# Down-projection units issued one pair of hidden tiles later, with two of four weight-block sums made by adding DMAs

## The chip, the cores and the metric

The kernel runs on one core of a Trainium2 chip. The metric is device time in microseconds (us) of one execution of the whole kernel, a decoder layer on 512 tokens of width 1024. Several executions are timed, and the median is given. Beside these there is one profiled execution, from which the trace and its page come.

## What is computed

The layer has two feed-forward blocks, one at its start and one at its end, with a token mixer and a memory attention between them. Only the feed-forward blocks are touched by the change:

```python
def swiglu(x, w1, w3, w2):
    return (jax.nn.silu(x @ w1) * (x @ w3)) @ w2

h = layer_norm(ALPHA * h + 0.5 * swiglu(h, ffn1_w1[l], ffn1_w3[l], ffn1_w2[l]), ln1_g[l], ln1_b[l])
...
h = layer_norm(ALPHA * h + 0.5 * swiglu(h, ffn2_w1[l], ffn2_w3[l], ffn2_w2[l]), ln4_g[l], ln4_b[l])
```

All is float32. `h` is 512 x 1024, `w1` and `w3` are 1024 x 2816, and `w2` is 2816 x 1024. The 2816 hidden columns are 22 tiles of 128, which the kernel takes in 11 pairs.

## The kernel before, in words

**Exact products.** A float32 operand is split into a high part and a low part in `float32r` (`split`: the copy that rounds, then a subtraction for the rest), and each product is three matmuls (`mm3`). The copy may go to ACT or to DVE (`scaled`), the subtraction is always on DVE. So every weight tile passes through DVE before TensorE can use it.

**Seven products in place of eight.** In the feed-forward blocks a 2 x 2 block product is done in Winograd's form with seven block products and sums of blocks. `Unit` (line 485) makes the seven weight forms of one unit, numbered 1 to 7, out of four loaded blocks of 128 x 1024: block 0 alone is form 1, block 2 form 2, block 3 form 3, and forms 5, 6, 7 and 4 are sums, made on DVE in place (block 0 takes in 1, then 3, then 2, and block 1 takes in 3). `Weights` keeps at most five such split tiles (`hl`) ahead of the product that TensorE is at, and `Unit.make` starts the loads of the unit after it at its fourth and its sixth form.

**Two kinds of units.** An up unit (`seven`, `products`) makes one pair of hidden tiles, with 7 products of 24 matmuls of 256 columns. Its outputs pass through ACT (silu) and DVE into a tile `G`. A down unit (`Forms`, `down7`) takes two pairs `G`, forms seven operands `A1` to `A7` out of their blocks (four of them sums on DVE, all split like weights), and makes 7 products of 12 matmuls of 512 columns, in banks dx, dy and dz. There are five down units, g = 0 to 4, over pairs 0 to 9; pair 10 goes through a plain product with `w2` (`res.add`), which ends the block and starts its layer norm.

**Order.** Pair 0 is made in another way at the block's start. Then the program issues, for g = 0 to 4, the up units of pairs 2g and 2g + 1, then down unit g, then the up unit of pair 10:

```python
        for g in range(5):
            if g:
                yield from seven(2 * g)
            forms = Forms(g)
            yield from seven(2 * g + 1, {4: lambda: forms.make(1, 2)})
            yield from down7(g, forms)
```

So down unit g follows at once on the up unit whose `G` it reads. The operands A1 and A2 are asked for ahead of the last product of that up unit, and the others inside the down unit.

**Sums over the down units.** `add` (line 716) takes each product out of its banks. For g = 0 it goes, added to the old residual, into four tiles `acc` in DRAM. For g = 1 to 4 ACT copies it to a staging tile `st` and POOL issues a DMA that adds it to `acc`; adds to the same `acc` wait for one another. `load_acc` reads `acc` back ahead of the fifth product of the up unit of pair 10, for the last sums.

**What sets the order on the engines.** A planner in the program (`Issue`) decides in which order DVE, ACT, POOL and SP (which issues the loads) get their instructions, by its own costs; each engine then works strictly in that order. All loads into SBUF go through SP's one queue. The blocks, `G`, `A`, `st` and `acc` share 20 slots of 4 KB per partition (`arena`), so a load waits where its slot is still in use. Small tables for the mixer (`tables`, line 1390) are made in the middle of the first block.

Of the kernel before, what the change touches and what calls it, by code (L numbers as in the profile page):

```python
# [13 lines left out]
ALU = mybir.AluOpType  # L14
# [4 lines left out]
P = 128  # L19
# [175 lines left out]
def layer(ctx: ExitStack, tc: tile.TileContext, a: dict, out: bass.AP):  # L195
# [247 lines left out]
    class Residual:  # L443
# [5 lines left out]
        def load(self):  # L449
            self.acc = [slot(f"acc{self.n}_{t}", F32, [P, D]) for t in range(NT)]  # L450
            for t in range(NT):
                sp.dma_start(self.acc[t], self.src[t * P:(t + 1) * P])
# [32 lines left out]
    class Unit:  # L485
# [2 lines left out]

        def __init__(self, name, src, order):
            self.name, self.src, self.order, self.after, self.b = name, src, order, None, {}  # L490

        def load(self, *blocks):
            for i in blocks:
                if i not in self.b:
                    self.b[i] = slot(f"{self.name}_b{i}", F32, [P, 1024])
                    for w in range(2):
                        sp.dma_start(self.b[i][:, w * 512:w * 512 + 512], self.src[i][w])

        def plan(self):
            for i in self.order:  # L500
# [2 lines left out]
        def make(self, i, hl):  # L503
            b, at = self.b, self.order.index(i)
            if at == 0:
                self.load(0, 1, 3, 2)
            if self.after and at in (3, 5):
                self.after.load(*((0, 1) if at == 3 else (3, 2)))
            for at, other in {5: ((0, 1),), 6: ((0, 3),), 7: ((1, 3),), 4: ((0, 2),)}.get(i, ()):
                dve.tensor_tensor(b[at], b[at], b[other], op=ALU.add)  # L510
            src = b[{1: 0, 5: 0, 6: 0, 4: 0, 3: 3, 7: 1, 2: 2}[i]]
            split(hl[:, 0], hl[:, 1], src)
            if i == 4:
                b.clear()

# [84 lines left out]
    def plan_ffn(n, w1, w3, w2):  # L600
        for f in range(2):
            W.plan(f"w1_{n}_{f}", w1[f])
            W.plan(f"w3_{n}_{f}", w3[f])

        def up(p):
            return Unit(f"wp{n}_{p}", [[w[2 * p + i % 2][:, i // 2 * 512:i // 2 * 512 + 512] for w in (w1, w3)] for i in range(4)], ORDER)

        def down(g):
            return Unit(f"wd{n}_{g}", [[w2[f * P:(f + 1) * P, i % 2 * 512:i % 2 * 512 + 512] for f in (4 * g + i // 2 * 2, 4 * g + i // 2 * 2 + 1)]
                                       for i in range(4)], DOWN)  # L610

        units = [up(1), down(0)]
        for g in range(1, 5):
            units += [up(2 * g), up(2 * g + 1), down(g)]
        units.append(up(10))
        for u, v in zip(units, units[1:]):
            u.after = v
        for u in units:
            u.plan()
        for f in (20, 21):  # L620
            W.plan(f"w2_{n}_{f}", w2[f * P:(f + 1) * P])

    def ffn(n, src, ready=None):
# [82 lines left out]
        def down7(g, forms):  # L706
# [7 lines left out]
                W.done(f"wd{n}_{g}_{i}")  # L714

            def add(pss, h, c, sign, new=False):
                if g == 0 and new:
                    st = old.pop((h, c))
                    for t in range(2):
                        dve.scalar_tensor_tensor(st[:, t], st[:, t], ALPHA, pss[t], op0=ALU.mult, op1=ALU.add if sign > 0 else ALU.subtract)  # L720
# [7 lines left out]
            x = [bank(f"dx{n}_{g}_{t}") for t in range(2)]  # L728
            product(x, 1, True)
            add(x, 0, 0, 1.0, True)  # L730
            forms.make(5, 6)
            yield
            y = [bank(f"dy{n}_{g}_{t}") for t in range(2)]
            product(y, 2, True)
# [32 lines left out]
            mark = sums_of_h(n, sums)  # L767
            yield from up(range(2))
        yield mark
        load_old()  # L770
        for g in range(5):
            if g:
                yield from seven(2 * g)
            forms = Forms(g)
            yield from seven(2 * g + 1, {4: lambda: forms.make(1, 2)})
            yield from down7(g, forms)

        def load_acc():
            res.acc = [slot(f"acc{n}_{t}", F32, [P, D]) for t in range(NT)]
# [1 line left out]
                for c in range(2):  # L781
                    sp.dma_start(res.acc[t][:, c * 512:c * 512 + 512], acc[t // 2, c][t % 2 * P:t % 2 * P + P])

        yield from seven(10, {7: load_acc})
        yield from res.add(lambda i, t: hl_of(gT[20 + i], slice(t * P, (t + 1) * P)), [f"w2_{n}_{f}" for f in (20, 21)], False, True)


# [707 lines left out]
```

## Time and profile before

| | us |
|---|---|
| median of 3 runs (1308.3 to 1309.8) | 1308.88 |
| profiled execution, its time | 1306.86 |
| profiled execution, its span | 1305.0 |
| first feed-forward block, first up unit to the first product of the mixer | 33.5 to 389.3 |
| mixer and memory attention | 389.3 to 954.7 |
| second block, first up unit to the end | 954.7 to 1305.0 |

Shares of the span in which an engine is busy: TensorE (PE) 94%, VectorE (DVE) 80%, ScalarE (ACT) 42%, GpSimd (POOL) 8%. These are averages over stages that differ; in both feed-forward blocks DVE is near its limit while TensorE has short pauses. Times in the trace are from the span's start. The page leaves out buffer numbers, so `wp_b` are the blocks of all up units and `wd_b` those of all down units. Almost all work has the line of a helper (L178 records it, L260 is the matmul), so it is told apart by its tiles.

### The profile page before, as it was taken

The page shows a single profiled execution, that of the slowest core. Times are in us where ns is not written, and L with a number is a line of the kernel's source. Part 1 is how long each engine was busy: PE and PEld are TensorE (multiplying, and loading weights), DVE is VectorE, ACT ScalarE, POOL GpSimd, SP SyncE. Part 2 cuts the span into 40 slices and gives each one's busy share as a digit, 9 for nine tenths or more (in the row PEclk, how much of TensorE's full clock was granted, in tenths as well). Part 3 has the DMA queues.
Part 4 walks back from the last instruction along what each step waited for, and adds up shares of the span by engine and source line. Part 5 has one row for each costly group of instructions (what it writes and reads, how often), then busy time and mean ns, then how long its engine had stood idle before and what let it go on. Part 6 is the DMA issues. An engine that isn't in the chain of part 4 may idle for free.

```text
span 1305.0 us, 19366 instructions
## 1 busy us (share of the span) xinstructions
PE 1229.0 (94%) x7530; PEld 1079.6 (83%) x7530; DVE 1038.6 (80%) x1603; ACT 551.3 (42%) x977; POOL 99.4 (8%) x95
## 2 busy tenths in 40 slices
PE   7898989899969999999999999999998989899995
PEld 6898988788859987877778898888996979797975
DVE  8999898789873699666666684574999898998987
ACT  5253434353532377433441243451544353535352
POOL 0010202020201100000000000000001020202020
PEclk9999999899989999999999999999999999999998
DMA  9381929484853321242333445234735474748374
GB/s 335 124 261 39 256 61 216 101 198 110 154 177 94 110 72 33 62 133 85 94 98 97 178 162 161 67 128 161 253 118 152 156 182 126 194 114 203 104 127 147
DMA packets 82879, 184.14 MB, mean 141 GB/s; under 512 B 8259, under 2 KB 10051, under 8 KB 82788
## 3 DMA queue, kind: packets, MB, share of 16 engines
q1 hardware_dynamic: 65924, 150.40, 34.3%
q0 software_dynamic: 16864, 32.51, 14.9%
q8 instruction: 59, 0.97, 0.3%
q14 instruction: 32, 0.26, 0.1%
HBM read 137.13 MB, written 45.74 MB: 140 GB/s over the span
## 4 chain that ended last, share of the span: by engine, by line
PE 70%; DVE 19%; DMA 4%; ACT 3%; issue 3%; SPq 0%; POOL 0%; DVEq 0%; POOLq 0%; ACTq 0%
PE pxwp L260 13%; PE pzwp L260 7%; DVE wd_hl L178 6%; PE dx L260 6%; PE dz L260 4%; PE mq L260 3%; PE res_w_o L260 3%; PE pgd L260 3%; PE res_mem_w_o L260 3%; DVE wd_b L178 2%; PE pywp L260 2%; PE pw L260 2%; PE mk L260 2%; PE vd L260 2%; PE pw_gm L260 2%
## 5 line engine op out<-in xcount | busy, mean ns | idle before, releaser
L178 DVE TENSOR_TENSOR wp_hl<-wp_b,wp_hl 128x1024 fp32r<-128x1024 f32 x140 | 168.9, 1222 | 15.6 <-ACT wp_hl L178 14.7
L178 ACT CAST wp_hl<-wp_b 128x1024 fp32r<-128x1024 f32 x88 | 92.1, 1052 | 82.1 <-PE pxwp L260 34.9
L260 PE MATMUL dx<-wd_hl,A 128*128 128x512 f32 x480 | 121.7, 399 | 2.4 <-DVE A L178 1.1
L170 POOL DMA_DIRECT2D acc<-st x62 | 77.6, 1478 | 600.5 <-ACT st L178 435.1
L260 PE MATMUL pxwp<-hT,wp_hl 128*128 128x256 f32 x960 | 121.1, 282 | 1.1 <-ACT wp_hl L178 0.4
L260 PE MATMUL pzwp<-S,wp_hl 128*128 128x256 f32 x960 | 121.8, 283 | 0.3 <-DVE S L178 0.3
L260 PE MATMUL pxwp<-S,wp_hl 128*128 128x256 f32 x960 | 122.0, 283 | 0.0
L260 PEld LDWEIGHTS pxwp<-hT,wp_hl 128*128 128x128 f32 x960 | 117.1, 188 | 5.5 <-DVE p_wp L178 2.1
L260 PEld LDWEIGHTS pzwp<-S,wp_hl 128*128 128x128 f32 x960 | 117.9, 191 | 0.5 <-DVE S L178 0.5
L260 PEld LDWEIGHTS pxwp<-S,wp_hl 128*128 128x128 f32 x960 | 118.1, 191 | 0.2 <-ACT p_wp L178 0.2
L260 PEld LDWEIGHTS dx<-wd_hl,A 128*128 128x128 f32 x480 | 88.9, 190 | 26.6 <-DVE A L178 7.6
L178 DVE TENSOR_TENSOR wd_hl<-wd_b,wd_hl 128x1024 fp32r<-128x1024 f32 x70 | 85.0, 1223 | 16.5 <-ACT wd_hl L178 16.3
L178 DVE TENSOR_TENSOR wp_b<-wp_b,wp_b 128x1024 f32<-128x1024 f32 x80 | 97.5, 1221 | 0.3
L260 PE MATMUL dz<-wd_hl,A 128*128 128x512 f32 x240 | 62.6, 400 | 12.2 <-ACT A L178 12.2
L260 PEld LDWEIGHTS dz<-wd_hl,A 128*128 128x128 f32 x240 | 43.7, 189 | 27.4 <-ACT A L178 15.9
L260 PE MATMUL pywp<-hT,wp_hl 128*128 128x256 f32 x480 | 60.0, 280 | 0.3 <-ACT wp_hl L178 0.3
L260 PE MATMUL dy<-wd_hl,A 128*128 128x512 f32 x120 | 37.1, 460 | 22.7 <-ACT A L178 17.7
L260 PEld LDWEIGHTS pywp<-hT,wp_hl 128*128 128x128 f32 x480 | 58.0, 188 | 0.5 <-ACT wp_hl L178 0.5
L260 PE MATMUL pw<-hT,w_hl 128*128 128x256 f32 (+1 forms) x288 | 50.2, 335 | 6.6 <-ACT hT L178 6.4
L260 PEld LDWEIGHTS pw<-hT,w_hl 128*128 128x128 f32 x288 | 43.0, 197 | 13.1 <-ACT hT L178 7.1
L260 PEld LDWEIGHTS dy<-wd_hl,A 128*128 128x128 f32 x120 | 24.9, 219 | 34.2 <-ACT A L178 21.5
L178 ACT ACTIVATE st<-dx 128x512 f32<-128x512 f32 x68 | 39.8, 598 | 22.9 <-PE dx L260 22.7
(329 smaller groups left out, 2332.0 us busy)
## 6 DMA issues: line engine op xcount, KB each, us to landing
wp_b<-in_ffn_w SPq DMA_DIRECT2D x160, 256.0 KB, 5.6
acc<-st POOLq DMA_DIRECT2D x62, 512.0 KB, 9.5
wd_b<-in_ffn_w SPq DMA_DIRECT2D x80, 256.0 KB, 6.8
h_dram<-acc SPq DMA_DIRECT2D x12, 512.0 KB, 3.0
w_raw<-in_ffn_w SPq DMA_DIRECT2D x11, 512.0 KB, 5.0
w_gm_raw<-in_w_gate SPq DMA_DIRECT2D x8, 512.0 KB, 5.8
acc<-old SPq DMA_DIRECT2D x8, 512.0 KB, 4.2
acc<-acc SPq DMA_DIRECT2D x16, 256.0 KB, 5.6
```

The costliest lines, as they stand in the source:

```text
L170: return (name, 1000.0, 4000.0, lambda: getattr(engine, op)(*args, **kw)), args[:1], list(args)
L178: return (name, ns, 1500.0 if name == "sync" else 0.0, lambda: getattr(engine, op)(*args, **kw)), outs, ins
L260: issue.pe(lambda: nc.tensor.matmul(ps, w, x, start=start, stop=stop, skip_group_check=again), ps, w, x)
```

## The change

- The order becomes: for g = 0 to 4 the up units of pairs 2g + 1 and 2g + 2, then down unit g. A down unit now reads two pairs of which the later was finished one up unit before. `res.add` for pair 10 follows on down unit 4, and no up unit stands between them.
- The operands A1, A2 and A5 are asked for inside the second up unit, ahead of its products 3, 2 and 4.
- Down unit 4 adds its products straight into the `acc` tiles in SBUF on DVE. Its 7 adding DMAs and 14 ACT copies per block are gone, and 14 additions of 128 x 512 on DVE are there. `load_acc` moves to the head of the up unit of pair 10.
- A down unit loads five blocks where it loaded four: block 4 is a second copy of block 0. POOL issues two DMAs that add in SBUF: block 1 from DRAM onto block 4 (form 5) and block 3 onto block 1 (form 7). Of the four sums on DVE two are left (forms 6 and 4). Each block is one DMA of 512 KB in place of two of 256 KB.
- In up units the blocks are loaded in the order 1, 0, 3, 2, where it was 0, 1, 3, 2.

```diff
@@ Unit @@
+            self.adds = not isinstance(src[0], list)
+
+        def move(self, i, block, add=False):
+            src = self.src[i]
+            if add:
+                pool.dma_start(block.rearrange("p (w c) -> p w c", w=2), src, accum_op=ALU.add)
+            elif isinstance(src, list):
+                for w in range(2):
+                    sp.dma_start(block[:, w * 512:w * 512 + 512], src[w])
+            else:
+                sp.dma_start(block.rearrange("p (w c) -> p w c", w=2), src)
 
         def load(self, *blocks):
+
             for i in blocks:
-                if i not in self.b:
+                if i not in self.b and (i < 4 or self.adds):
                     self.b[i] = slot(f"{self.name}_b{i}", F32, [P, 1024])
-                    for w in range(2):
-                        sp.dma_start(self.b[i][:, w * 512:w * 512 + 512], self.src[i][w])
+                    self.move(i % 4, self.b[i])
+                    if self.adds and i in (1, 4):
+                        self.move(3 if i == 1 else 1, self.b[i], True)
...
             if at == 0:
-                self.load(0, 1, 3, 2)
+                self.load(4, 1, 0, 3, 2)
             if self.after and at in (3, 5):
-                self.after.load(*((0, 1) if at == 3 else (3, 2)))
-            for at, other in {5: ((0, 1),), 6: ((0, 3),), 7: ((1, 3),), 4: ((0, 2),)}.get(i, ()):
-                dve.tensor_tensor(b[at], b[at], b[other], op=ALU.add)
-            src = b[{1: 0, 5: 0, 6: 0, 4: 0, 3: 3, 7: 1, 2: 2}[i]]
+                self.after.load(*((4, 1, 0) if at == 3 else (3, 2)))
+            t = 4 if self.adds else 0
+            src = b[{1: 0, 5: t, 6: t, 4: t, 3: 3, 7: 1, 2: 2}[i]]
+            other = {5: 1, 6: 3, 7: 3, 4: 2}.get(i)
+            if other is not None and not (self.adds and i in (5, 7)):
+                dve.tensor_tensor(src, src, b[other], op=ALU.add)
             split(hl[:, 0], hl[:, 1], src)
+            if i == 1 and self.adds:
+                del b[0]
@@ plan_ffn @@
-        units = [up(1), down(0)]
-        for g in range(1, 5):
-            units += [up(2 * g), up(2 * g + 1), down(g)]
-        units.append(up(10))
+        units = []
+        for g in range(5):
+            units += [up(2 * g + 1), up(2 * g + 2), down(g)]
@@ ffn: down7 @@
             def add(pss, h, c, sign, new=False):
-                if g == 0 and new:
+                if g == 4:
+                    for t in range(2):
+                        dst = res.acc[2 * h + t][:, c * 512:c * 512 + 512]
+                        dve.tensor_tensor(dst, dst, pss[t], op=ALU.add if sign > 0 else ALU.subtract)
+                elif g == 0 and new:
...
-            forms.make(5, 6)
+            forms.make(6)
@@ ffn: the order @@
         for g in range(5):
-            if g:
-                yield from seven(2 * g)
+            yield from seven(2 * g + 1)
             forms = Forms(g)
-            yield from seven(2 * g + 1, {4: lambda: forms.make(1, 2)})
+            late = {3: lambda: forms.make(1), 2: lambda: forms.make(2), 4: lambda: forms.make(5)}
+            if g == 4:
+                late[1] = load_acc
+            yield from seven(2 * g + 2, late)
             yield from down7(g, forms)
...
-        yield from seven(10, {7: load_acc})
```

Three places show how the instructions move.

**VectorE, first block, around the start of down unit 2.** The names are tile, block, unit: `wd1_2_b1` is block 1 of down unit 2, `wd1_2_7_hl` its split form 7, `G1_5` the output of the up unit of pair 5, `A2_1_2` the operand A2, `Sa` to `Sd` the sums for the operands. Before:

```order
L178 TENSOR_TENSOR wd1_2_3_hl_1822<-wd1_2_b3_1627,wd1_2_3_hl_1822 128x1024
L178 TENSOR_TENSOR wd1_2_b1_1560<-wd1_2_b1_1560,wd1_2_b3_1627 128x1024
L178 SCALAR_TENSOR_TENSOR G1_5_1600<-p1_wp1_5_1629,G1_5_1600 128x256
L178 CAST wd1_2_7_hl_1843<-wd1_2_b1_1560 128x1024
L178 SCALAR_TENSOR_TENSOR G1_5_1600<-pxwp1_5_1601,G1_5_1600 128x256
L178 TENSOR_TENSOR A2_1_2_1797<-G1_5_1600,A2_1_2_1797 128x2x256
L178 TENSOR_TENSOR wd1_2_7_hl_1843<-wd1_2_b1_1560,wd1_2_7_hl_1843 128x1024
L178 TENSOR_TENSOR wd1_2_b0_1559<-wd1_2_b0_1559,wd1_2_b2_1628 128x1024
L178 TENSOR_TENSOR Sa_1_2_1847<-G1_5_1600,G1_4_1375 128x512
L178 CAST wd1_2_4_hl_1878<-wd1_2_b0_1559 128x1024
L178 TENSOR_TENSOR Sd_1_2_1906<-G1_4_1375 128x512
L178 TENSOR_TENSOR A5_1_2_1848<-Sa_1_2_1847,A5_1_2_1848 128x2x256
```

With the change:

```order
L178 TENSOR_TENSOR Sa_1_2_2023<-G1_5_1597,G1_4_1190 128x512
L178 TENSOR_TENSOR wd1_2_1_hl_1916<-wd1_2_b0_1783,wd1_2_1_hl_1916 128x1024
L178 SCALAR_TENSOR_TENSOR Sb_1_2_2076<-Sa_1_2_2023,G1_4_1190 128x512
L178 CAST wd1_2_2_hl_1946<-wd1_2_b2_1852 128x1024
L178 TENSOR_TENSOR u2_wp1_6_1917<-u2_wp1_6_1917,pzwp1_6_1861 128x512
L178 TENSOR_TENSOR wd1_2_2_hl_1946<-wd1_2_b2_1852,wd1_2_2_hl_1946 128x1024
L178 SCALAR_TENSOR_TENSOR G1_6_1824<-u2_wp1_6_1917,G1_6_1824 128x256
L178 CAST wd1_2_5_hl_1976<-wd1_2_b4_1781 128x1024
L178 TENSOR_TENSOR A2_1_2_1983<-G1_5_1597,A2_1_2_1983 128x2x256
L178 TENSOR_TENSOR wd1_2_5_hl_1976<-wd1_2_b4_1781,wd1_2_5_hl_1976 128x1024
L178 TENSOR_TENSOR p5_wp1_6_1887<-p5_wp1_6_1887,pxwp1_6_1825 128x512
L178 TENSOR_TENSOR wd1_2_b4_1781<-wd1_2_b4_1781,wd1_2_b3_1851 128x1024
```

Before, A2 and the sum Sa stand behind the last write of `G1_5`, and the sums of blocks 1 and 0 between them; now Sa, Sb and A2 stand among the weights of the down unit, `G1_6` is written for a later unit, and form 5 is split out of block 4 with no sum on DVE.

**TensorE, first block, its end.** `res1_w2` are the last products, with the token tile and the half behind them; `trh1` are the transposes of the normed tiles, one token tile each, and `pw_gm` the first products of the mixer, whose first half needs token tiles 0 and 1 only. Before:

```order
L260 MATMUL res1_w2_1_20_3_0_3636<-w2_1_20_hl_3390,g1_20_3531 128x512 x3
L260 MATMUL res1_w2_1_20_3_0_3636<-w2_1_21_hl_3421,g1_21_3456 128x512 x3
L260 MATMUL res1_w2_1_20_3_1_3646<-w2_1_20_hl_3390,g1_20_3531 128x512 x3
L260 MATMUL res1_w2_1_20_3_1_3646<-w2_1_21_hl_3421,g1_21_3456 128x512 x3
L269 MATMUL trh1_1_0_3680<-ident_84,acc1_1_3427 128x128 x4
L269 MATMUL trh1_1_1_3685<-ident_84,acc1_1_3427 128x128 x4
L269 MATMUL trh1_2_0_3697<-ident_84,acc1_2_3428 128x128 x4
L269 MATMUL trh1_2_1_3702<-ident_84,acc1_2_3428 128x128 x4
L260 MATMUL pw_gm0_3671<-hT0_89,w_gm0_hl_3455 128x256
L260 MATMUL pw_gm1_3672<-hT0_89,w_gm1_hl_3497 128x256
```

With the change:

```order
L260 MATMUL res1_w2_1_20_3_1_3604<-w2_1_20_hl_3424,g1_20_3351 128x512 x3
L260 MATMUL res1_w2_1_20_3_1_3604<-w2_1_21_hl_3446,g1_21_3282 128x512 x3
L269 MATMUL trh1_0_0_3637<-ident_84,acc1_0_3119 128x128 x4
L269 MATMUL trh1_0_1_3642<-ident_84,acc1_0_3119 128x128 x4
L269 MATMUL trh1_1_0_3651<-ident_84,acc1_1_3120 128x128 x4
L269 MATMUL trh1_1_1_3657<-ident_84,acc1_1_3120 128x128 x4
L269 MATMUL trh1_2_0_3681<-ident_84,acc1_2_3121 128x128 x4
L269 MATMUL trh1_2_1_3686<-ident_84,acc1_2_3121 128x128 x4
L269 MATMUL trh1_3_0_3695<-ident_84,acc1_3_3122 128x128 x4
L269 MATMUL trh1_3_1_3700<-ident_84,acc1_3_3122 128x128 x4
L260 MATMUL pw_gm0_3625<-hT0_89,w_gm0_hl_3469 128x256 x12
```

Before, the transposes of tiles 0 to 2 are mixed with the last products and the mixer starts ahead of those of tile 3; now all transposes stand in a row behind the last product, and the mixer starts behind the last of them.

**POOL, first block, the adding DMAs between down units 1 and 2** (`acc1_0_1` is the tile in DRAM for token half 0 and column half 1). Before:

```order
L170 DMA acc1_0_1_115<-st1_1_0_1_1296 128x2x512
L170 DMA acc1_0_1_115<-st1_1_0_1_1320 128x2x512
L170 DMA acc1_1_1_117<-st1_1_1_1_1342 128x2x512
L170 DMA acc1_1_0_116<-st1_1_1_0_1368 128x2x512
L170 DMA acc1_0_0_114<-st1_2_0_0_1846 128x2x512
L170 DMA acc1_0_0_114<-st1_2_0_0_1879 128x2x512
```

With the change:

```order
L170 DMA acc1_0_1_115<-st1_1_0_1_1521 128x2x512
L170 DMA acc1_0_1_115<-st1_1_0_1_1544 128x2x512
L170 DMA acc1_1_1_117<-st1_1_1_1_1566 128x2x512
L170 DMA acc1_1_0_116<-st1_1_1_0_1590 128x2x512
L170 DMA wd1_2_b4_1781<-in_ffn1_w2 128x2x512
L170 DMA wd1_2_b1_1782<-in_ffn1_w2 128x2x512
L170 DMA acc1_0_0_114<-st1_2_0_0_2075 128x2x512
```

The two adds for the weights of down unit 2 stand behind all adds of down unit 1 and ahead of those of unit 2.

## Rows read from the trace of the kernel before

**Rows 1.** The page: its head and the busy time of each engine.

```profile
span 1305.0 us, 19366 instructions
...
PE 1229.0 (94%) x7530; PEld 1079.6 (83%) x7530; DVE 1038.6 (80%) x1603; ACT 551.3 (42%) x977; POOL 99.4 (8%) x95
```

**Rows 2.** Stretches: stretch, length, PE, PEld, DVE, ACT, POOL busy (count); PEclk, DMA, GB/s.

```profile
144.00:184.00 40.00, 39.91 (x335) 39.67 (x334) 35.12 (x42) 12.82 (x20) 4.04 (x3) 1.00 0.62 177
184.00:208.00 24.00, 20.70 (x90) 15.58 (x89) 23.31 (x29) 14.75 (x25) 4.81 (x4) 1.00 0.61 123
248.00:279.00 31.00, 26.08 (x103) 20.00 (x102) 27.91 (x34) 15.50 (x26) 5.06 (x4) 0.83 0.57 159
```

**Rows 3.** Timeline of TensorE: first or last products of up units (start, length, what).

```profile
33.52 3.01 PE L260 MATMUL pxwp<-hT,wp_hl 128*128 128x256 f32 x24
...
144.15 3.02 PE L260 MATMUL pxwp<-hT,wp_hl 128*128 128x256 f32 x24
...
208.21 3.02 PE L260 MATMUL pxwp<-hT,wp_hl 128*128 128x256 f32 x24
...
360.00 2.98 PE L260 MATMUL pxwp<-hT,wp_hl 128*128 128x256 f32 x24
...
954.73 3.01 PE L260 MATMUL pxwp<-hT,wp_hl 128*128 128x256 f32 x24
...
1277.49 2.98 PE L260 MATMUL pxwp<-hT,wp_hl 128*128 128x256 f32 x24
```

**Rows 4.** Timeline of TensorE in down unit 2 of the first block [idle before].

```profile
184.46 1.07 PE L260 MATMUL dx<-wd_hl,A 128*128 128x512 f32 x4
...
189.53 3.03 PE L260 MATMUL dy<-wd_hl,A 128*128 128x512 f32 x12 [1.72 <-ACT A L178]
...
194.00 3.21 PE L260 MATMUL dz<-wd_hl,A 128*128 128x512 f32 x12 [1.43 <-ACT A L178]
```

**Rows 5.** Chain of waits, in order of time, in two down units (start, length, what).

```profile
187.36 1.13 DVE wd_b L178
...
264.93 2.73 PE dz L260 x12
```

**Rows 6.** Groups by line and tile: count | busy us, mean ns | idle before.

```profile
L178 DVE TENSOR_TENSOR wd_b<-wd_b,wd_b 128x1024 f32<-128x1024 f32 x40 | 48.8, 1223 | 0.3
...
L178 DVE CAST wd_hl<-wd_b 128x1024 fp32r<-128x1024 f32 x45 | 30.9, 690 | 0.0
...
L178 DVE SCALAR_TENSOR_TENSOR acc<-acc,res_w 128x512 f32<-128x512 f32 x16 | 10.9, 683 | 5.0 <-PE res_w L260 5.0
```

**Rows 7.** Issue to landing: first adds acc<-st (512 KB), then loads wd_b (256 KB).

```profile
DMA to landing us min/median/max: 5.8/9.5/15.7
...
DMA to landing us min/median/max: 3.9/6.8/15.0
```

**Rows 8.** POOL: its adds by group, then its timeline near the end of down unit 2.

```profile
L170 POOL DMA_DIRECT2D acc<-st x62 | 77.6, 1478 | 600.5 <-ACT st L178 435.1 <-DMA acc<-st 67.5 <-ACT A L178 64.1
...
201.09 1.20 POOL L170 DMA_DIRECT2D acc<-st  x1 [0.70 <-ACT st L178]
...
212.50 4.04 POOL L170 DMA_DIRECT2D acc<-st  x3 [10.21 <-ACT wp_hl L178]
```

**Rows 9.** Timelines of SP, PE and DVE at the ends of both blocks.

```profile
337.85 21.25 SPq L178 DMA_DIRECT2D acc<-acc  x8
...
369.78 10.10 PE L260 MATMUL res_w<-w_hl,g 128*128 128x512 f32 x36 [6.80 <-DVE g L178]
...
373.54 0.69 DVE L178 SCALAR_TENSOR_TENSOR acc<-acc,res_w 128x512 f32<-128x512 f32 x1 [3.09 <-PE res_w L260]
...
389.28 7.32 PE L260 MATMUL pw_gm<-hT,w_gm_hl 128*128 128x256 f32 x60
...
396.54 1.09 PE L269 MATMUL trh<-ident,acc 128*128 128x128 f32 x8
...
1284.01 0.69 DVE L178 SCALAR_TENSOR_TENSOR acc<-acc,res_w 128x512 f32<-128x512 f32 x1 [1.48 <-PE res_w L260]
```

More of the change, by code (lines that the diff above doesn't have):

```diff
@@ L608, in down @@
         def down(g):
-            return Unit(f"wd{n}_{g}", [[w2[f * P:(f + 1) * P, i % 2 * 512:i % 2 * 512 + 512] for f in (4 * g + i // 2 * 2, 4 * g + i // 2 * 2 + 1)]
-                                       for i in range(4)], DOWN)
-        units = [up(1), down(0)]
-        for g in range(1, 5):
-            units += [up(2 * g), up(2 * g + 1), down(g)]
-        units.append(up(10))
+            rows = [w2[f * P:(f + 2) * P].rearrange("(f p) c -> p f c", p=P) for f in (4 * g, 4 * g + 2)]
+            return Unit(f"wd{n}_{g}", [rows[i // 2][:, :, i % 2 * 512:i % 2 * 512 + 512] for i in range(4)], DOWN)
+        units = []
+        for g in range(5):
+            units += [up(2 * g + 1), up(2 * g + 2), down(g)]
         for u, v in zip(units, units[1:]):
@@ L769, in ffn @@
         yield mark
-        load_old()
-        for g in range(5):
-            if g:
-                yield from seven(2 * g)
-            forms = Forms(g)
-            yield from seven(2 * g + 1, {4: lambda: forms.make(1, 2)})
-            yield from down7(g, forms)
         def load_acc():
@@ L782, in load_acc @@
                     sp.dma_start(res.acc[t][:, c * 512:c * 512 + 512], acc[t // 2, c][t % 2 * P:t % 2 * P + P])
-        yield from seven(10, {7: load_acc})
+        load_old()
+        for g in range(5):
+            yield from seven(2 * g + 1)
+            forms = Forms(g)
+            late = {3: lambda: forms.make(1), 2: lambda: forms.make(2), 4: lambda: forms.make(5)}
+            if g == 4:
+                late[1] = load_acc
+            yield from seven(2 * g + 2, late)
+            yield from down7(g, forms)
         yield from res.add(lambda i, t: hl_of(gT[20 + i], slice(t * P, (t + 1) * P)), [f"w2_{n}_{f}" for f in (20, 21)], False, True)
```

## The prediction

> **What bounds the kernel now.** I read first the busy time of each engine [rows 1]. TensorE is busy for 1229.0 of 1305.0 us, so at most 76 us of pauses are to be had in the whole kernel. DVE's 80% is an average and hides its stages, so the second view is that of the stretches [rows 2]. While two up units run (144 to 184), TensorE is busy for 39.91 of 40 us and DVE for 35.12: the products are the bound. In the down unit behind them (184 to 208) TensorE is busy for only 20.70 of 24 us, and DVE for 23.31: there DVE is the bound. The third view, TensorE's timeline of that down unit [rows 4], says what the pauses wait for: dy waits 1.72 us and dz 1.43 us for an `A`, together 3.15 of the 3.3 us of pause. The chain of waits [rows 5] runs at that moment through a weight-block sum on DVE (1.13 us at 187.36). So the operands A2 and A5 are late, since `G` of the up unit just before ends with that unit, and their sums then queue on DVE between the splits and sums of the weights. The clock adds to it: in the stretch from 248 to 279, another down unit, the granted clock is 0.83, and it takes 31 us in place of 24 [rows 2].
>
> **How much is lost.** Two up units take 184.46 - 144.15 = 40.31 us [rows 3, 4], 20.16 each. A product of a down unit that waits for nothing takes 2.73 us [rows 5], seven 19.11. A period of two up units and one down unit would be 59.43 us; it is 208.21 - 144.15 = 64.06 us [rows 3]. A block has ten up units and five down units from the first up unit to the last product of pair 10: 10 x 20.16 + 5 x 19.11 = 297.1 us. The first block takes 33.52 to 362.98, 329.5 us, the second 954.73 to 1280.47, 325.7 us [rows 3]. Lost are 32.4 and 28.6 us, 61.0 in all, about 6 per down unit.
>
> **The order: later down units.** The later `G` that a down unit reads is now complete one up unit (20 us) before it begins, and the operands 1, 2 and 5 are made inside that up unit. The waits for `A` should go, and with them the slower clock that followed. The amount of work is the same; it moves out of the stretch in which DVE is full into one where it had 40 - 35.12 = 4.9 us free.
>
> **DVE.** Its load in a period was 35.12 + 23.31 = 58.4 us [rows 2]. Two sums of 1.223 us go, 2.4 us [rows 6]. In the new order of DVE and ACT, 27 copies of down weights move from DVE to ACT and 13 of up weights come back, 14 fewer over ten periods, at 0.690 us [rows 6] 1.0 us each period. Left are 55.0 of 59.4 us, 93%: it fits, with 4.4 us free. ACT takes those copies with some 27 of 59 us in use now (12.82 + 14.75), so I cost them at nothing; if ACT had no room, the price would be the copies' 1.0 us a period again. As DVE works strictly in order and is still at 93%, I do not give the whole loss back: I leave the length of one sum, 1.2 us, in each of the ten down units, 12 us. The bounds are 0 (nothing waits) and 3.0 (half of the loss stays).
>
> **The adding DMAs.** No DMA of the trace before adds onto a weight block; the nearest rows are the adds to `acc`, of the same 512 KB and issued by POOL too. They land after 5.8 to 15.7 us, median 9.5, and loads of blocks after 3.9 to 15.0, median 6.8 [rows 7]. Count from T, the end of a down unit (208.21). Its fourth add is issued at 201.09 [rows 8], lands at T + 2.4 and frees the staging slots; the block loads, issued at about T + 4, land at T + 11. POOL takes its queue in order: the last adds of the down unit end at 212.50 + 4.04, T + 8.3 [rows 8], so the two new ones wait for the loads alone. Issued at T + 12, they land at T + 22. Form 5, the first that needs one, may be split five products ahead of its own, which is when four products of the second up unit are done: T + 20.16 + 4 x 2.88 = T + 31.7. The margin is 9.7 us; I cost the DMAs at nothing, hidden by the up units. With the longest times of the rows for both steps they land at T + 4 + 15.0 + 1.2 + 15.7 = T + 36, 4 us late, still within the 4.4 us that DVE has free. The further bound is the rival below. SP is asked for the same loads plus one block more per unit, 512 KB, while the DMA engines are busy at about 0.6 [rows 2].
>
> **Down unit 4 and the ends of the blocks.** Its 14 additions on DVE (0.683 us, by the nearest row, which also reads a bank [rows 6]) are 9.6 us; the weights of a next up unit, which DVE made there in the other periods, are not there. I take 1 us for them in the second block. In the first, the span from the last product of pair 10 to the mixer's first product was 389.28 - 362.98 = 26.3 us, of which 6.80 was a wait for `g` [rows 9], in a time when SP was held for 21.25 us by the reload of `acc`; that reload is now asked for ahead of down unit 4. What remains counts from the end of down unit 4: first sum of `acc` after 3.76 us (369.78 to 373.54), from there to the transposes of the last token tile 23.0 us (to 396.54), and these 1.09, since the mixer now stands behind them: 27.9 us. That is 1.6 more; 1.1 comes back, as those transposes interrupted the mixer before. For the additions and two splits of mixer weights that stand ahead on DVE (2 x 1.22) I add 2.5. So the first end loses 3.0 us and the second 1.0. The bounds for both are a gain of 2 (the wait of 6.80 was worth more) and a loss of 10 (the 9.6 us of additions all come late once).
>
> **The sum.** 61.0 - 12 - 3.0 - 1.0 = 45.0 us gained. The profiled execution took 1306.86 us, so 1261.9; the median of the runs, 1308.88, is 2.0 higher: **1264 us**. A measurement here can tell about 0.2%, 2.6 us, from no change.
>
> **Rivals.**
> *DVE stays the bound.* Half of the loss stays, 3.0 us per down unit in place of 1.2, since splits and operands still take turns on a DVE that is 93% busy: 18 us more, 1282 us. For it: 23.31 of 24 us before. Against it: the work is now spread over the whole period. Chance 0.17.
>
> *The adding DMAs come late.* DVE then stands at form 5, and everything behind it on DVE stands too: splits, `G`, operands. If the adds wait so long on POOL's side that form 5 is 7 us late in each unit, that is 2.6 us beyond the free 4.4, 26 us in all, 1290 us. For it: the adds of before already spread from 5.8 to 15.7 us, and their issues on POOL took 1478 ns on average against 1.20 us for one alone [rows 7, 8]. Against it: the margin of 9.7 us, so that two landings must take some 17 us more than the medians together. Chance 0.10. The Trainium skill ("SBUF — State Buffer", section "SBUF: two separate sides") speaks against the change here: while DVE copies float32 within SBUF, GpSimd is shut out of a shared port and cannot write the descriptors of the DMAs that POOL issues; the page gives about 620 ns for such a DMA alone and 3100 ns beside a copy. By that page an estimate would be 2.5 us more for each add, 5 us in a unit. The trace agrees that adds beside a busy DVE are slow to land and spread widely, but no run here has shown them beside an idle one.
>
> *SP's queue is held* (slower). The blocks, three `G`, the operands and `st` share 20 slots; a down unit now wants five blocks. If a load at the head of SP's queue waits for a slot that an adding DMA has to free, the blocks of the next up unit stand behind it. Five split tiles ahead cover 5 x 2.88 = 14.4 us. From a hold of 14.4 + 4.5 = 18.9 us per period on, the gain of 4.5 per period is gone; a hold as long as that of `load_acc`, 21.25 us [rows 9], costs 6.9 us ten times, 69 - 45 = 24 us slower: 1333 us. For it: such a hold stands in the trace. Against it: fewer `st` slots are in use in down unit 4, and in the middle of a block no up unit waits for blocks now (39.91 of 40). Chance 0.07.
>
> *Nothing gained.* The pauses in the down units are the clock's and not the operands': then the order changes nothing, 1309 us. Against it: unit 2 has the same waits at a clock of 1.00 [rows 2, 4]. Chance 0.04.
>
> **How the numbers follow.** The forecast keeps 0.62. Faster by over 0.2%: 0.62 + 0.17 + 0.10 = 0.89; within: 0.04; slower: 0.07. The range runs from 1249 (no remainder in the down units, 1 us lost at the ends: 60 us gained) to 1290, which takes in both rivals that are still faster, and with them the bounds of the remainder and of the ends; left out are the last two rivals, 0.11, and a little of the rest.
>
> **What would show it.** Right: periods of 59 to 61 us; in the down units no wait of dy or dz for `A`; a granted clock of 1.00 in the stretch that answers to 248 to 279; TensorE busy for about 97% of the span; the new adds landing after about 9.5 us, with no wait of `wd_hl` on DVE for them; no 6.80 us wait ahead of `res_w`. Wrong: waits of DVE for the adding DMAs at form 5 (second rival), TensorE waiting for `wp_hl` while SP's queue is held (third), or waits of `dx` to `dz` for `wd_hl` on a full DVE (first).

## The result and the profile after

The changed kernel takes 1261.59 us (median of 4 runs, 1261.37 to 1263.0), the kernel before 1309.08 in the same session: a ratio of 0.964, 95% interval 0.9623 to 0.9656. It is faster by 47.5 us; 1264 was forecast, with a range of 1249 to 1290. The profiled execution's span is 1259.7 us, 45.3 below that of before [rows 1].

The page of the changed kernel, its head, the busy time of each engine, and the landing times of the DMAs of the down units (count, KB, median us):

```profile
span 1259.7 us, 19354 instructions
...
PE 1214.5 (96%) x7530; PEld 1080.1 (86%) x7530; DVE 1019.4 (81%) x1590; ACT 551.0 (44%) x970; POOL 105.5 (8%) x101
...
wd_b<-in_ffn_w SPq DMA_DIRECT2D x50, 512.0 KB, 10.0
acc<-st POOLq DMA_DIRECT2D x48, 512.0 KB, 9.9
wd_b<-in_ffn_w POOLq DMA_DIRECT2D x20, 512.0 KB, 12.9
```

As many instructions, 7530, keep TensorE busy for 14.5 us less, and its pauses fell from 76.0 to 45.2 us. Down blocks in one DMA of 512 KB land after 10.0 us, the new adds on them after 12.9.

Stretches of the first block (length, then PE, PEld, DVE, ACT, POOL busy with counts, granted clock, DMA share, GB/s), the first two of one undisturbed period, the third of the one behind it, the last of the down unit at the end of that one:

```profile
153.00:190.00 37.00, 37.00 (x313) 37.00 (x312) 33.10 (x40) 13.94 (x22) 6.26 (x5) 1.00 0.98 249
190.00:212.00 22.00, 22.00 (x111) 18.71 (x110) 21.60 (x27) 14.93 (x24) 5.26 (x4) 1.00 0.50 104
...
212.00:284.00 72.00, 65.48 (x426) 57.91 (x425) 54.59 (x70) 30.09 (x47) 10.93 (x9) 0.93 0.78 176
...
262.00:284.00 22.00, 21.52 (x95) 16.37 (x95) 21.86 (x27) 14.62 (x24) 4.83 (x4) 1.00 0.59 114
```

These answer to [rows 2]: in the down unit (190 to 212) TensorE is now busy for all of 22 us, where it was 20.70 of 24, though DVE is still at 21.60. In the third stretch it pauses for 6.5 us, and the mean clock is 0.93; in the down unit at its end, which answers to 248 to 279, the clock is 1.00 where it was 0.83. Waits of TensorE, by what ended them (total us, times, longest), of before:

```profile
PE dy L260 <- ACT A L178: 17.7, 9, 3.4
PE dz L260 <- ACT A L178: 12.2, 8, 2.1
...
PE dy L260 <- DVE A L178: 3.5, 2, 1.8
...
PE trh L269 <- DVE acc L178: 3.2, 2, 1.8
...
PE dx L260 <- DVE A L178: 1.1, 5, 0.5
PE dx L260 <- ACT A L178: 1.0, 1, 1.0
```

and of the changed kernel:

```profile
PE trh L269 <- DVE acc L178: 9.3, 2, 6.0
...
PE rel L260 <- DMA hot<-in_onehot: 4.4, 1, 4.4
```

The 35.5 us of waits for `A` are gone (17.7 + 12.2 + 3.5 + 1.1 + 1.0), and so is the wait for `g` of [rows 9]. New is the wait for the onehot table `hot`; that of the transposes for `acc`, both times at the end of the first block, has grown from 3.2 to 9.3 us. TensorE's timeline of the changed kernel (start, length, what) shows the period and the ends:

```profile
152.96 3.02 PE L260 MATMUL pxwp<-hT,wp_hl 128*128 128x256 f32 x24
...
212.03 3.01 PE L260 MATMUL pxwp<-hT,wp_hl 128*128 128x256 f32 x24
216.66 0.74 PE L260 MATMUL pxwp<-S,wp_hl 128*128 128x256 f32 x4 [1.62 <-ACT p_wp L178]
221.81 2.30 PE L260 MATMUL rel<-hot,rel 33*8 33x320 f32 x4 [4.41 <-DMA hot<-in_onehot]
224.04 5.13 PE L260 MATMUL pzwp<-S,wp_hl 128*128 128x256 f32 x24
...
283.94 3.02 PE L260 MATMUL pxwp<-hT,wp_hl 128*128 128x256 f32 x24
...
346.68 9.23 PE L260 MATMUL res_w<-w_hl,g 128*128 128x512 f32 x40
...
372.13 13.15 PE L260 MATMUL pw_gm<-hT,w_gm_hl 128*128 128x256 f32 x110
...
936.26 3.01 PE L260 MATMUL pxwp<-hT,wp_hl 128*128 128x256 f32 x24
...
1238.18 9.23 PE L260 MATMUL res_w<-w_hl,g 128*128 128x512 f32 x40
```

A period without disturbance is 212.03 - 152.96 = 59.07 us, where it was 64.06 [rows 3]. The next one is 283.94 - 212.03 = 71.9 us: most of what is left of the loss in the first block stands there.

The table gives for each kernel of this study the time from the first dy product of one down unit to that of the next, from TensorE's timeline of its profiled execution, and from the last one of block 2 to the end of the span ("between" runs from the last down unit of block 1 to the first of block 2). It shows where in the kernel a change acts, with one caution: where a dy matmul slips ahead of the last product of the up unit, the mark stands 2.8 us earlier, as in order_only:

```profile
1229.81 0.39 PE L260 MATMUL dy<-wd_hl,A 128*128 128x512 f32 x1
1230.03 3.02 PE L260 MATMUL pxwp<-hT,wp_hl 128*128 128x256 f32 x24
```

The medians are of five sessions, in which the kernel before took 1309.1 to 1311.1 us; the ratios are against the kernel before in the same session.

| kernel | block 1 | between | block 2 | to the end | span | median |
|---|---|---|---|---|---|---|
| before | 65.5, 64.0, 64.3, 70.3 | 656.9 | 68.4, 64.0, 64.1, 64.0 | 63.4 | 1305.0 | 1309.1 |
| changed | 60.7, 59.1, 70.2, 60.9 | 653.5 | 60.7, 59.1, 59.1, 59.1 | 41.4 | 1259.7 | 1261.6 |
| order_only | 64.8, 56.6, 74.0, 61.8 | 657.8 | 64.9, 56.5, 59.9, 59.8 | 47.0 | 1276.8 | 1278.2 |
| adds_only | 66.2, 62.9, 66.0, 65.0 | 658.7 | 64.6, 62.0, 62.0, 62.9 | 62.8 | 1293.1 | 1294.2 |
| g4_by_dma | 60.7, 59.1, 68.2, 60.9 | 666.2 | 60.7, 59.1, 59.1, 59.1 | 57.2 | 1286.2 | 1289.9 |
| adds_in_4 | 64.9, 56.5, 74.6, 65.1 | 652.1 | 64.9, 56.5, 60.0, 62.6 | 41.3 | 1271.3 | 1272.4 |
| asked_late | 61.0, 59.1, 68.9, 60.0 | 658.7 | 61.0, 59.1, 59.1, 57.2 | 45.3 | 1266.3 | 1268.5 |
| adds_held | 66.2, 59.7, 70.0, 70.4 | 655.9 | 68.5, 59.2, 62.4, 66.7 | 41.9 | 1298.1 | 1298.1 |
| adds_late | 60.8, 59.1, 70.3, 60.9 | 653.9 | 60.8, 59.1, 59.1, 59.1 | 41.3 | 1260.7 | 1261.4 |
| tab160 | 60.7, 62.5, 62.0, 59.1 | 653.7 | 60.7, 59.0, 59.1, 59.1 | 41.2 | 1252.8 | 1255.0 |
| tab160_one | 60.7, 62.5, 62.1, 59.1 | 653.6 | 60.7, 59.1, 59.1, 59.1 | 41.3 | 1253.1 | 1254.7 |
| tab_split | 60.8, 61.0, 63.5, 67.1 | 653.8 | 60.8, 59.1, 59.1, 59.2 | 41.3 | 1262.7 | 1264.8 |
| tab_split_one | 60.7, 60.4, 62.9, 63.8 | 654.4 | 60.7, 59.1, 59.1, 59.2 | 41.3 | 1258.5 | 1260.6 |
| tab_mixer | 60.7, 59.3, 59.1, 59.1 | 664.3 | 60.7, 59.1, 59.1, 59.1 | 41.3 | 1258.8 | 1258.5 |

### The profile page after: what moved, and what is told of

Read it like the earlier page. It is cut to its first block, busy times and chain, and to the rows that moved or that the text cites. A ratio compares the mean times of both kernels' runs of the same rounds, so it can differ in the third digit from the quotient of the medians.

```text
span 1259.7 us, 19354 instructions
## 1 busy us (share of the span) xinstructions
PE 1214.5 (96%) x7530; PEld 1080.1 (86%) x7530; DVE 1019.4 (81%) x1590; ACT 551.0 (44%) x970; POOL 105.5 (8%) x101
## 5 line engine op out<-in xcount | busy, mean ns | idle before, releaser
L178 DVE TENSOR_TENSOR wp_hl<-wp_b,wp_hl 128x1024 fp32r<-128x1024 f32 x140 | 168.2, 1220 | 12.9 <-ACT wp_hl L178 10.6
L178 ACT CAST wp_hl<-wp_b 128x1024 fp32r<-128x1024 f32 x75 | 78.7, 1051 | 93.3 <-PE pxwp L260 51.6
L260 PE MATMUL dx<-wd_hl,A 128*128 128x512 f32 x480 | 117.4, 391 | 1.6 <-DVE acc L178 1.2
L170 POOL DMA_DIRECT2D acc<-st x48 | 59.5, 1561 | 379.7 <-ACT st L178 205.1
L178 ACT CAST wd_hl<-wd_b 128x1024 fp32r<-128x1024 f32 x52 | 54.5, 1052 | 54.5 <-PE pxwp L260 24.9
L260 PE MATMUL dz<-wd_hl,A 128*128 128x512 f32 x240 | 59.2, 392 | 0.5 <-ACT st L178 0.3
L178 DVE CAST wp_hl<-wp_b 128x1024 fp32r<-128x1024 f32 x65 | 46.1, 710 | 7.4 <-PE pzwp L260 6.1
L260 PE MATMUL pgd<-hT,w_gd_hl 128*128 128x512 f32 x192 | 47.5, 400 | 0.0
## 6 DMA issues: line engine op xcount, KB each, us to landing
wd_b<-in_ffn_w POOLq DMA_DIRECT2D x20, 512.0 KB, 12.9
```

The lines of the kernel that those rows point to most:

```text
L170: return (name, 1000.0, 4000.0, lambda: getattr(engine, op)(*args, **kw)), args[:1], list(args)
L178: return (name, ns, 1500.0 if name == "sync" else 0.0, lambda: getattr(engine, op)(*args, **kw)), outs, ins
L260: issue.pe(lambda: nc.tensor.matmul(ps, w, x, start=start, stop=stop, skip_group_check=again), ps, w, x)
```

## The experiments

The theory was that late operands cost the time; the main rival, that DVE's load in the down units did.

**The order alone** (order_only). `Unit` and `down` as before, the rest as changed:

```diff
-            self.adds = not isinstance(src[0], list)
...
-            t = 4 if self.adds else 0
+            for at, other in {5: ((0, 1),), 6: ((0, 3),), 7: ((1, 3),), 4: ((0, 2),)}.get(i, ()):
+                dve.tensor_tensor(b[at], b[at], b[other], op=ALU.add)
```

> The changed kernel with the down units' blocks loaded and summed as before (four blocks in eight DMAs, four sums on DVE, no adding DMA on weights); the new order, the early operands and down unit 4 stay. Theory (the late operands cost the time): the waits of dy and dz for A stay away; DVE gets 2.4 us per period back on top of some 55 of 59, 97%, which costs at most 1.2 us in each of ten down units: 1262 to 1274 us. Rival (DVE's load in the down units was the bound, and the adding DMAs lifted it): half of the gain or more is gone, 1285 us or more, with TensorE waiting for weights in the down units.

Measured: 1278.19 us, ratio 0.9754 (0.9736 to 0.9771): two thirds of the gain, between the two expectations. TensorE's waits for `A` fell from 35.5 us to these two:

```profile
PE dx L260 <- DVE A L178: 2.6, 2, 2.2
```

In an undisturbed period (block 2, the last two) it takes 59.9 us against 59.1 with the adds and 64.1 before, so 4.2 of the 5.0 us are the order's. Most of the rest of its loss is elsewhere: 5.6 us behind the last down unit (2.8 of them the mark's), 4.3 between the blocks, 3.8 in the period with the tables.

**The adds alone** (adds_only). The kernel before with the changed `Unit` and `down`:

> The kernel before with the new loads and adding DMAs of the down units alone; order, operands and down unit 4 as before. Theory: A2 and A5 still come after the last output of the up unit just before, so the waits of dy and dz for A stay; 2.4 us less on DVE in the down unit gives back at most that of some 6 us, ten times: 1285 to 1309 us. Rival (DVE's load was the bound): most of the gain comes, 1275 us or less.

Measured: 1294.24 us, ratio 0.9868 (0.9851 to 0.9884), within what the theory expected. The undisturbed periods of block 2 fall by 2 us, and TensorE still waits for `A`:

```profile
PE dy L260 <- ACT A L178: 10.2, 9, 2.9
PE dy L260 <- DVE A L178: 6.1, 7, 0.9
...
PE dz L260 <- ACT A L178: 4.6, 3, 2.1
...
PE dz L260 <- DVE A L178: 2.8, 1, 2.8
```

32 us of the order and 16 of the adds make up the 48 of both. The totals add up, the parts do not: in an undisturbed period 4.2 us of the order and 2.0 of the adds are more than the 5.0 of both, and the order alone loses at the ends of the blocks. This run also has the single DMAs of 512 KB and the new order of the up units' blocks; the next one shows what these are worth.

**Where the adds pay** (adds_in_4): adding DMAs in down unit 4 of each block alone.

```diff
-            self.adds = not isinstance(src[0], list)
+            self.adds = not isinstance(src[0], list) and "_4" in name
```

> The changed kernel with adding DMAs on weights in down unit 4 of each block alone; in the other eight down units the four sums are on DVE (blocks still in single DMAs of 512 KB). The run with all sums on DVE was 16 us slower than the changed kernel on its span, of which 5.6 us lay behind down unit 4 of the second block, 4.3 between the two blocks, 3 to 6 inside each block. Theory (the adding DMAs pay where DVE also has the 14 additions, at the ends of the blocks): 8 to 10 us come back, 1266 to 1272 us. Rival (they pay evenly, some 1.6 us per down unit): only 3 us come back, 1274 to 1279 us.

Measured: 1272.37 us, ratio 0.9709 (0.9693 to 0.9726); 5.8 us came back, between the two. By the table the two ends are 5.7 us shorter each than in order_only, and the periods that lead into down unit 4 are 3.3 and 2.8 longer. That is the mark: here the last up product stands ahead of all dy products of down unit 4 again. Some 2.9 us are left for each end. So the adds do pay where DVE has the 14 additions too, though less than the theory had. The other down units have single DMAs of 512 KB here, and the up units the new order of blocks, and their undisturbed periods are those of order_only (64.9, 56.5, 60.0): with the new order of units, these two gain nothing by themselves.

**Down unit 4 through DRAM** (g4_by_dma):

```diff
-                if g == 4:
-                    for t in range(2):
-                        dst = res.acc[2 * h + t][:, c * 512:c * 512 + 512]
-                        dve.tensor_tensor(dst, dst, pss[t], op=ALU.add if sign > 0 else ALU.subtract)
-                elif g == 0 and new:
+                if g == 0 and new:
...
             yield from down7(g, forms)
+        load_acc()
```

> The changed kernel with down unit 4 like the others: its products go through st and adding DMAs on POOL, and acc is read back behind the last of them. Theory (the additions in SBUF pay): the first sum of acc waits for copy, add (9.9 us) and reload (about 6), some 17 us against 3.8 now, at the ends of both blocks: 10 to 14 us each, 1282 to 1290 us. Rival (the 14 additions on DVE cost as much as the way through DRAM did): 1256 to 1267 us.

Measured: 1289.9 us, ratio 0.9838 (0.9823 to 0.9852). The table has 12.7 us more between the blocks and 15.8 more at the end; both waits of its trace stand in that way:

```profile
PE trh L269 <- DVE acc L178: 23.8, 2, 17.9
...
DVE acc L178 <- DMA acc<-acc: 38.0, 6, 11.7
```

So the additions in SBUF are no ornament of the new order but its condition: with a down unit last in the block, the way through DRAM is on the path.

**The operands asked for as before** (asked_late):

```diff
-            forms.make(6)
+            forms.make(5, 6)
...
-            late = {3: lambda: forms.make(1), 2: lambda: forms.make(2), 4: lambda: forms.make(5)}
+            late = {4: lambda: forms.make(1, 2)}
```

> The changed kernel with the operands asked for as before: A1 and A2 ahead of the last product of the second up unit, A5 and A6 in the down unit. The pair that a down unit reads is still one up unit old. Theory (that G is complete earlier is what counts): at most 0.6 us per down unit, 1260 to 1268 us. Rival (asking for them earlier is what counts, as DVE's queue is full in the down unit): waits of dy and dz for A come back, 1275 us or more.

Measured: 1268.51 us, ratio 0.9682 (0.9668 to 0.9697), just above the theory's 1268. Undisturbed periods keep their 59.1 us; what is lost stands at the ends (5.2 between the blocks, 3.9 behind the last unit, less the 0.9 and 1.9 by which the periods ahead are shorter). There the operands of down unit 4 now share DVE with the 14 additions, which would explain it; no run tries it by itself. For a steady period it is `G` being a unit older that counts, not the asking.

**How far the adds are hidden.** In adds_late the adds were asked for at form 1 in place of with the loads:

> The changed kernel with the two adding DMAs of a down unit asked for when its form 1 is made and not with the loads, some 10 us later; the same work. Theory (they are hidden by a margin of about 10 us ahead of form 5, and DVE has 4 us free): form 5 now comes 3 to 7 us late in each unit, DVE waits for wd_b there, and 0 to 3 us are lost ten times: 1268 to 1292 us. Rival (the margin is much larger, since the tiles ahead of TensorE cover the wait): 1259 to 1265 us.

It measured 1261.37 us, but says nothing of the margin: the adds of down unit 2 started at 166.03 in place of 165.28, as they stand behind the same loads and the same adds to `acc` on POOL either way. So in adds_held they were made to depend on form 1:

```diff
-                    if self.adds and i in (1, 4):
-                        self.move(3 if i == 1 else 1, self.b[i], True)
...
             if i == 1 and self.adds:
+                held = vec(f"{self.name}_held")
+                pool.tensor_tensor(held, f32(hl[:, 1, 0:1]), f32(hl[:, 1, 0:1]), op=ALU.subtract)
+                for t in (b[4], b[1]):
+                    pool.tensor_tensor(t[:, :1], t[:, :1], held, op=ALU.add)
+                self.move(1, b[4], True)
+                self.move(3, b[1], True)
                 del b[0]
```

> The changed kernel with the two adding DMAs of a down unit held on POOL until form 1 of that unit is split, by three tiny additions of zero that the DMAs depend on. (Asking for them later in the program, the run before, had not moved their start: 165.28 us in down unit 2 of the first block with the change, 166.03 there.) In the changed kernel form 1 of that unit is split at 184.0 us and form 5 is copied at 187.48. With some 2.5 us for the three additions and a landing after 4 to 13 us, form 5 comes at 191 to 200, 4 to 12 us late. Theory (the adds are free for as long as they land ahead of form 5, and DVE has 4 us of a period to give): about 4 us are lost in each of ten down units, 1285 to 1320 us, with waits of DVE for wd_b. Rival (the split tiles ahead of TensorE cover such a wait): 1259 to 1270 us.

Measured: 1298.05 us, ratio 0.9903 (0.9878 to 0.9928): 36 us lost. Its waits on DVE:

```profile
DVE wd_hl L178 <- DMA wd_b<-in_ffn_w: 35.9, 10, 4.9
```

Ten waits, 3.6 us each in the mean, stand beside 38 us more span. That the two sums are nearly alike gives no price for a wait: by the table the undisturbed periods of block 2 grew by 0.1, 3.3 and 7.6 us. The adds to `acc` behind them on POOL were held too, and no run tells their part. So the second rival is a real mechanism, and here it cost more than the rival's sum would give, which put a lateness of up to 4.4 us at nothing; whether DVE's free time took in a part stays open. In the changed kernel it doesn't come up: DVE nowhere waits for one of these adds.

**The period with the tables.** On SP (loads, then its waits for adding DMAs from 200 to 217), then on DVE, around its start in the changed kernel:

```profile
200.66 14.75 SPq L178 DMA_DIRECT2D wp_b<-in_ffn_w  x8
215.51 0.37 SPq L178 DMA_DIRECT2D hot<-in_onehot  x1
215.98 0.34 SPq L178 DMA_DIRECT2D lam<-in_lam  x1
...
SPq L178 <- DMA acc<-st: 10.6, 2, 7.8
...
222.12 0.29 DVE L178 TENSOR_TENSOR lam<-lam 128x128 f32<-128x128 f32 x1 [4.34 <-DMA lam<-in_lam]
```

`hot` is asked for only at 215.51, since the eight loads ahead of it on SP take 14.75 us; 10.6 of them go by waiting for adds to `acc`, which free the slots of `st`. TensorE has its product next in line and stands for 4.41 us, DVE has `lam` next and stands for 4.34, and nothing behind them moves. The list of the kernel before has no wait for `hot`. Then the clock falls (length, PE, PEld, DVE, ACT, POOL, granted clock):

```profile
212.00:221.00 9.00, 3.78 (x29) 3.34 (x27) 5.79 (x6) 3.41 (x4) 0.47 (x1) 0.85 0.98 239
221.00:229.00 8.00, 7.19 (x28) 5.32 (x29) 1.57 (x5) 0.20 (x1) 3.20 (x3) 0.53 0.93 147
229.00:240.00 11.00, 11.00 (x95) 11.00 (x94) 9.20 (x10) 3.83 (x5) 0.00 (x0) 1.00 0.88 183
```

At 0.53 a product of 24 matmuls takes 5.13 us (224.04, above) in place of 3.04. Five runs moved this work. tab160 plans it at 160 us:

```diff
-        mark.floor = 200000.0
+        mark.floor = 160000.0
```

> The changed kernel with the mixer's small tables planned at 160 us in place of 200, so that the load of the onehot table stands on SP behind the blocks of down unit 2 and not behind the held blocks of pair 8, and their product at the end of pair 5. Theory (the 12.9 us that the period from 212.03 is longer than the one ahead of it come from TensorE and DVE standing in line behind a late load, and from the slower clock after it): they go, 1248 to 1253 us. Rival (the tables' own work on PE, DVE and SP costs this wherever it stands): 1259 to 1264 us.

Measured: **1254.96 us**, ratio 0.9575 (0.956 to 0.9589), faster than both kernels, though short of the theory. The waits for `hot` and `lam` are gone; 6.3 us remain in the two periods there (62.5 and 62.0 against 59.1). Its loads on SP show why:

```profile
148.80 14.61 SPq L178 DMA_DIRECT2D wd_b<-in_ffn_w  x3
163.51 0.40 SPq L178 DMA_DIRECT2D hot<-in_onehot  x1
...
171.60 0.98 SPq L178 DMA_DIRECT2D wd_b<-in_ffn_w  x2
```

Blocks 3 and 2 of down unit 2 are asked for from 171.60 on in place of 163.08, and TensorE waits there for `A` again:

```profile
PE dy L260 <- ACT A L178: 1.7, 1, 1.7
```

To see whether slots or queue do that, tab160_one puts the three slots into one:

> The run with the tables at 160 us, with its three slots (onehot, lam, rows) put into one: the two loads share one 4 KB tile, and the results overwrite the onehot table. Nothing else moves. Theory (the 6 us that were still lost there, 62.5 and 62.0 us against 59.1, came from slots that the blocks of down unit 2 lacked): they go or halve, 1248 to 1252 us. Rival (the place in the queues costs it, not the slots): 1254 to 1257 us.

It measured 1254.65 us, ratio 0.9574 (0.9557 to 0.9591), with the same periods (62.5, 62.1), as its rival had it. But slots are not cleared by it. Its loads of blocks 3 and 2 on SP, and what SP waited for between them:

```profile
164.26 8.73 SPq L178 DMA_DIRECT2D wd_b<-in_ffn_w  x2
...
SPq L178 <- DMA acc<-st: 7.9, 1, 7.9
```

With two slots back, block 3 goes out at 164.26 again; block 2 still waits 7.9 us for a slot that an add to `acc` frees. One slot too few holds the last block as long as three do; whether the queue has a part stays open. tab_split loads the tables behind all those blocks, at 165 us, and uses them at 178:

> The changed kernel with the tables' loads planned at 165 us (on SP behind all blocks of down unit 2, ahead of those of pair 7) and their products at 178 us, just ahead of down unit 2. With the tables at 160 us the wait for them was gone, but their slots held up two blocks of down unit 2 and 6 us were lost there. Theory: the blocks stand ahead now, and those 6 us go: 1247 to 1251 us. Rival (the slots that the tables hold are missed by the up unit's blocks instead): 1253 to 1262 us.

Measured: 1264.76 us, ratio 0.9651 (0.9637 to 0.9666), no faster than the changed kernel, whose interval overlaps. On SP the write of the results goes out at 199.88, and the next pair's blocks behind it only from 218.85 on, after a wait of 18.1 us for an add to `acc`; the changed kernel asks for them from 200.66 on. With one slot:

> The run with the tables' loads behind all blocks of down unit 2 and their products at the end of pair 6 (1264.8 us), with its three slots put into one. Theory (slots): its loss of 13.7 us in the periods after the second (63.5 and 67.1 against 59.1, and 61.0) falls to a third or less, 1250 to 1256 us. Rival (the write of the results, which stands on SP ahead of the blocks of pair 8 and waits for them): 1260 to 1266 us.

it took 1260.61 us, ratio 0.9621 (0.9607 to 0.9635): so two slots make 4 us of it. The wait of SP there is still 14.7 us for an add to `acc`; what the write's place in the queue adds was not tried by itself. tab_mixer moves loads and products into the mixer:

> The changed kernel with the onehot and lam loads planned at 345 us, at the very end of the first block, and their products at 385 us in the mixer, where TensorE is busy all the time and DVE for 6 to 13 of 28 to 30 us; only the loads of the constants stay at 200 us. Theory (the period with the tables is 70.2 us because their loads, slots and their place in the in-order queues cost it 11 us): the period comes down to 59 to 60 and the mixer grows by 1 to 3: 1248 to 1253 us. Rival (the slots or queues of the mixer are as tight): 1256 us or more.

Measured: 1258.46 us, ratio 0.9597 (0.9575 to 0.9618). The first block is then free of it (238.2 us for four periods, where the changed kernel has 250.9), but the stretch between the blocks grew by 10.8, so nearly all of the gain was given back. What in the mixer costs that stays open. tab160 and tab160_one are the fastest here, 0.5% below the changed kernel, with intervals that don't meet its own.

## Why the prediction was right, and where it was not

**The order.** The forecast period was 59.43 us, and it is 59.07; the waits of dy and dz for `A` went, and the clock is 1.00 in undisturbed periods. TensorE is busy for 96% of the span, where about 97 was forecast. Both runs that undo a part agree: the order alone takes a period from 64.1 to 59.9, the adds alone to 62.0, with most of the waits of dy for `A` still there.

**DVE.** Forecast were 55.0 of 59.4 us in a period; it is 54.70 of 59.0 (33.10 + 21.60 in the two stretches above). The remainder of 1.2 us in each of ten down units is the step that was wrong in kind: four of the eight periods are at 59.1 us, with TensorE busy for all of 37 and of 22 us. What is left is in other places. The first rival has a part of the truth: DVE is at 21.60 of 22 us in a down unit, and with its two sums back (order_only) 0.8 us per period return. From the first up unit to the last product of down unit 4 (33.16 to 346.7, 936.26 to 1238.2), less 2.5 us of early `res_w`, the blocks take 311.0 and 299.4 us, 13.9 and 2.3 above the 297.1 of the sum: 16.2 in place of 12, and 11 of them are the period with the late load for the tables. That is the third rival's mechanism, a load on SP that waits for a slot that an adding DMA frees, in a place it had not named: split tiles stand ahead of TensorE for the blocks, but nothing does for a table. The kernel before has a long period at the end of its first block too (70.3), which was counted with the rest; what made it was not tried.

**The adding DMAs.** Issue was forecast at T + 12, with T = 152.96 here: the first add starts at 165.28, T + 12.3. Landing was taken from the adds to `acc`, 9.5 us; the median of the new adds is 12.9, and the two of this unit took 17.5 and 20.7. The issues of the new adds on POOL (min, median, max ns) and their landing in the whole kernel, the adds of this unit and their landing, and the copy of its form 5 on DVE:

```profile
L170 POOL DMA_DIRECT2D wd_b<-in_ffn_w x20: 1213/1270/3324, 40.4 to 1187.3; - x20
...
DMA to landing us min/median/max: 7.0/12.9/20.7
...
165.28 4.06 POOL L170 DMA_DIRECT2D wd_b<-in_ffn_w  x2
...
DMA to landing us min/median/max: 17.5/19.1/20.7
...
187.48 0.69 DVE L178 CAST wd_hl<-wd_b 128x1024 fp32r<-128x1024 f32 x1
```

Form 5 is copied at 187.48, T + 34.5, and its add landed at 165.28 + 17.5 = 182.8: the margin was 4.7 us where 9.7 stood, and it would have been 9.3 with the median landing. It held, though half of it was gone; adds_held shows that lateness costs. The rival's page of the Trainium skill ("SBUF — State Buffer", "SBUF: two separate sides") has copies on DVE delay the adds that POOL issues. The trace agrees as far as the adds land later than the forecast and some of their issues take up to 3324 ns; the median issue, 1270 ns, is close to the shortest. That DVE's copies are the cause, no run here shows. Another cause is as near, the load on the DMA engines: their share is 0.98 in the stretch from 153 to 190, and in adds_held, where the adds go out later and the share around those of this unit was 0.66, they landed after a median of 7.5 us; but DVE was busy for only 4.99 of 9.30 us there, so that run does not part the two.

**The ends.** Forecast were losses of 3.0 and 1.0 us. The first end took 372.13 - 346.68 + 2.5 = 28.0 us against 26.3, 1.7 lost; the second 1259.7 - 1238.18 + 2.5 = 24.0 against 24.5, 0.5 won. The additions were overpriced. One reason is that the adding DMAs had made room on DVE just there, which the sum had not seen: adds_in_4 is 5.8 us faster than order_only by them. The prediction gave the adds no price of their own; it took their two sums, 2.4 us a period, out of DVE's load, and asked only whether that fits. They were worth 16 us, a third of the gain.

**The sum.** 45.0 us of span were forecast and 45.3 came, but out of 44.8 in the blocks in place of 49.0, -1.2 at the ends in place of -4.0, and 1.7 in the mixer and the head that were in no term. The errors cancelled, so part of the closeness is luck: the total was better than its parts.

## What to carry to other kernels

Where an engine waits for an operand that is finished just before it is needed, in line with other work on a full engine, give it the length of a stage; and look at what then ends the block, as its latency becomes the path (27 us here without the additions in SBUF). Price an engine's load per stretch, not per period: two sums fewer were worth 0.8 us in a steady period and some 2.9 at each end. A period that is longer than its neighbours has a cause of its own; look for the late load before putting it down to the clock. And compare a mark between kernels only where the same work stands ahead of it.

## What the runs showed of the hardware

A DMA that adds 512 KB onto SBUF landed after 12.9 us (median, 7.0 to 20.7) beside 9.9 for the same size onto DRAM and 10.0 for a plain load; issued later in the period, in adds_held, the same adds landed after 7.5 us (5.7 to 9.1). After stops of 1.62 and 4.41 us TensorE's granted clock was 0.53 over the next 8 us, close to the lower of its two levels, and 1.00 behind that. A load on SP that waited 7.8 us for a slot held up the loads behind it on the same queue, and TensorE and DVE stood 4.41 and 4.34 us for two small ones among them.
